# Four inner projections and the cross queries computed feature-major, inputs laid out transposed, and a new order table, in a two-layer decoder trunk

## The chip, the cores and the metric

The kernel runs on one core of a Trainium2 chip. The metric is the time of one execution in microseconds (us), taken on the device. The engines are TensorE (PE, matrix products; PEld is its loading of stationary operands), VectorE (DVE), ScalarE (ACT), GpSimd (POOL) and SyncE (SP), which here issues nearly all transfers. Sums of products land in PSUM, a small memory of eight banks beside PE; everything else is in SBUF.

## The reference

Two decoder layers on x (1, 256, 1024) with a memory `mem` (1, 256, 1024), all float32. Each layer:

```
x = LN1(a*x + 0.5 * SwiGLU_1(x))                      # hidden width 2816
z = x @ w_in + b_in                                   # split into u, v, cb, cc, ch, the latents of MLA, the inputs of NSA, gates ga..gd
y_A = (u * (causal(w_s) @ LN(v) + b_s)) @ w_out       # gMLP: chunks of 128 tokens, 4 groups of 128 features
y_B = (cb * conv3(cc * ch)) @ w_out                   # gated short conv, 3 taps along the tokens, width 512
y_C = multi-head latent attention                     # MLA, 8 heads, causal
y_D = native sparse attention                         # NSA, 8 heads in 2 groups
x = LN2(a*x + (sum_i sigmoid(g_i) * y_i) @ w_o)
q, k, v = x @ wq, mem @ wk, mem @ wv                  # 4 heads of 128
x = LN3(a*x + softmax(q k^T / sqrt(128)) v @ wo)
x = LN4(a*x + 0.5 * SwiGLU_2(x))
```

## The kernel before

**Tiling.** The 256 tokens are two tiles of 128 (t = 0, 1). An activation is kept token-major (tokens on the 128 partitions) in `x[t]`, and once more transposed, feature-major, as `xh`, `xl` of tile t: eight blocks of 128 features, `xh` the value rounded to fp32r and `xl` the rest. Every weight comes from HBM once, as float32, in pieces of up to 512 KB: `unit` (L221) issues the transfer of a piece to `raw` on SP (L233), ACT rounds it to `wh` (L236) and DVE subtracts to `wl` (L237). There are 4 `raw` buffers and 8 pairs of `wh`, `wl`. A product is three matmuls, written out in `mm3` (L246): high by high (L248), high by low (L249), low by high (L250). They add into one PSUM tile.

**z and its transposes.** `z` (L407) computes a group of columns of x @ w_in token-major: for each t and each of eight k, a 128x128 block of `xh` is the stationary operand and 512 columns of weights move. The bias is a row of b_in that a transfer spreads over all partitions (256 KB for 512 columns); DVE adds it while it empties PSUM. Where a result is needed feature-major, PE transposes it: a matmul of 128 columns by the identity `ident`, four of them into one PSUM tile (`transposes`, L294; every such row of the trace has L298), and ACT and DVE split the copy into high and low. That is so for the product u * s of the gMLP (`zu`), for cc * ch (`zch`) and the gate cb (`zcb`) of the conv, for the cross queries (`xq`), for the merged sum of the branches (`T`, into `xh`, L286), for MLA's queries and keys (`mq`, `mk`), for softmax results (`e`), for the normalised x, and for x and mem as loaded (`memr`).

**Stages.** Of a layer: the first FFN (`ffn`, L366), `mixing` (L747) with its four branches a to d, gates and `w_o`, then the keys of mem (`xattn_k`, L873; 96 matmuls of 256 columns, the weights stationary and the transposed mem moving), LN2 (`layer_norm`), the cross attention (`xattn`, L900: queries for both t, scores, softmax, the values of mem in `xattn_v`, outputs, then `xattn_wo` through `wide`), LN3 and the second FFN with LN4. `run` (L941) loads x on SP in three parts after the first weight piece and transposes it on PE, four blocks of four.

**What sets the order.** The program is written stage by stage, and then each engine's instructions are put into the order of a table of numbers, `ISSUE` (L984), that holds for PE, ACT, DVE, POOL and SP: `issue_order` (L969) adds a dependence from each instruction to the next of its engine. Nothing is decided at run time; an instruction that waits holds up all that stand behind it on its engine.

Of the kernel before, what the change touches and what calls it, by code (L numbers as in the profile page):

```python
# [17 lines left out]
P = 128  # L18
# [43 lines left out]
IN_COLS, ZW = _in_columns()  # L62
WOUT_ROWS = np.arange(512).reshape(2, 4, 64).transpose(1, 0, 2).reshape(-1)
# [9 lines left out]
def _constants():  # L73
# [31 lines left out]
    for j in range(4):  # L105
# [24 lines left out]
        "b_in": IN_WIDTH, "gmlp_ln_g": 512, "gmlp_ln_b": 512, "mla_qnorm_g": 256, "mla_kvnorm_g": 128}  # L130
# [7 lines left out]
SMALL = {"ws": 512, "bs": 4, "cw": 12, "pek": 16, "pev": 16, "wck": 1024, "wcv": 1024}  # L138
# [18 lines left out]
DEFER = 3  # L157


class Build:  # L160
    def __init__(self, ctx, tc, aps):
# [10 lines left out]
        self.ident = self.p.tile([P, P], F32, name="ident")  # L172

# [47 lines left out]
    def unit(self, W, l, k0, nk, c0, w):  # L221
# [3 lines left out]
        with self.tc.high_priority(offset=WPRI):  # L225
# [3 lines left out]
            pieces = []  # L229
            for k in range(0, nk, kp):  # L230
                m = min(kp, nk - k) * w
# [6 lines left out]
                pieces.append((hi, lo))  # L238

        def get(k, n0, n1):  # L240
            i, r = divmod(k, kp)
            hi, lo = pieces[i]
            return hi[:, r * w + n0:r * w + n1], lo[:, r * w + n0:r * w + n1]
# [57 lines left out]
    def big(self, t, name, kt=KD):  # L301
        h = self.p.tile([P, KD, P], F32R, name=self.nm("xh"), tag=f"xh{t}", bufs=1)
        lo = self.p.tile([P, KD, P], F32R, name=self.nm("xl"), tag=f"xl{t}", bufs=1)
        return h, lo

    def to_xT(self, t, x, scale=1.0):
        h, lo = self.big(t, "x")
# [58 lines left out]
    def ffn(self, l, which, lnw, last=False):  # L366
# [3 lines left out]
        for gi in range(6):  # L370
            c0 = gi * 512
            w = min(512, FF - c0)
            if w == 512:
                u1 = self.cols(w1, l, c0, w, KD)
                u3 = self.cols(w3, l, c0, w, KD)
            else:
                u13 = self.cols((w1, w3), l, c0, 2 * w, KD)
            for t in range(NT):
                self.stream = "af"[t]
                if w == 512:  # L380
# [3 lines left out]
                else:  # L384
# [22 lines left out]
    def z(self, l, names, evac):  # L407
# [275 lines left out]
    def gmlp(self, l, S):  # L683
# [12 lines left out]
        def spatial(t):  # L696
            v, u = S["v", t], S["u", t]
            ps = self.acc()
            for i in range(4):
                nc.tensor.matmul(ps[:, i * P:(i + 1) * P], ws[:, i * P:(i + 1) * P], v[:, i * P:(i + 1) * P],  # L700
                                 start=True, stop=True, skip_group_check=True)
            for i in range(4):
                sl = slice(i * P, (i + 1) * P)
                nc.vector.scalar_tensor_tensor(u[:, sl], ps[:, sl], bs[:, i:i + 1], u[:, sl], op0=ALU.add,
                                               op1=ALU.mult)

        def turn(t):
            u = S["u", t]
            pt = self.transposes([u[:, i * P:(i + 1) * P] for i in range(4)])
            out[t] = self.pair("ya", pt)  # L710
        self.later += [lambda t=t, f=f: f(t) for f in (spatial, turn) for t in range(NT)]
        return out

    def conv(self, l, S):
        nc = self.nc
        cwv = S["cw"].rearrange("p (f k) -> p f k", f=4)
        out, Z = {}, {}

        def turn(t):
            zp = S["ch", t]  # L720
            nc.vector.tensor_mul(zp, zp, S["cc", t])
            pt = self.transposes([zp[:, i * P:(i + 1) * P] for i in range(4)])
            zt = self.p.tile([P, 4, P + 2], F32, name=self.nm("zpT"), tag="zpT", bufs=2)
            if t == 0:
                nc.vector.memset(zt[:, :, 0:2], 0.0)
            else:
                nc.vector.tensor_copy(zt[:, :, 0:2], Z[0][:, :, P:P + 2])
            nc.scalar.copy(zt[:, :, 2:], pt.rearrange("p (f t) -> p f t", f=4))
            Z[t] = zt

        def taps(t):
            zt = Z[t]
            y = self.s("y")
            yv = y.rearrange("p (f t) -> p f t", f=4)
# [433 lines left out]
```

## Time and profile before

| | |
|---|---|
| median of 3 runs | 1530.36 us (1526.17 to 1535.17) |
| the profiled execution | 1528.15 us, of which the span of the trace is 1526.4 us |
| PE busy | 1489.9 us, 98% of the span |
| DVE, ACT, POOL busy | 1002.8, 719.9 and 50.6 us |
| moved by DMA | 278.76 MB, 183 GB/s over the span |
| mean granted clock of PE | 0.997 |

The span runs from the first to the last instruction that the profiler saw. A row of the trace carries the line of the kernel, the operation, the tiles that it writes and reads, and in brackets the engine's idle time before it with what ended that. Matmuls overlap, so the duration in a row is longer than the distance between the starts of two rows; the distance is what a matmul costs.

### The profile page before, as it was taken

How to read it: one execution, taken by the hardware profiler on the slowest of the kernel's cores; microseconds unless marked ns; L12 is line 12 of the kernel's file. 1: busy time of each engine (PE TensorE's matmuls, PEld its weight loads, DVE VectorE, ACT ScalarE, POOL GpSimd, SP SyncE). 2: the span in 40 equal slices, each digit the busy share in tenths (PEclk: the TensorE clock that was granted, in tenths of full speed). 3: DMA queues.
4: the chain of work that ended last, by engine and by line, in shares of the span. 5: the costliest groups of instructions: out<-in, count | busy, mean ns of one | idle time of the engine just before them, and what ended most of it. 6: DMA issues, size and time to landing. Idle time of an engine off the chain costs nothing.

```text
span 1526.4 us, 20113 instructions
## 1 busy us (share of the span) xinstructions
PE 1489.9 (98%) x7606; PEld 1234.3 (81%) x7606; DVE 1002.8 (66%) x1426; ACT 719.9 (47%) x1060; POOL 50.6 (3%) x48
## 2 busy tenths in 40 slices
PE   8999999999999999999999999999999999999997
PEld 6888888877887888888878888888778878888886
DVE  5545478878866767554565556788887577765644
ACT  6435344555644454544345444355565444544541
POOL 0000001000120000000000000010001100000000
PEclk9999999999999999999999999999999999999999
DMA  7567557424475545566555666654245655356551
GB/s 275 163 222 238 192 185 243 139 90 151 151 235 204 181 162 166 178 196 206 166 193 183 197 213 201 219 202 159 98 139 185 221 193 193 124 195 205 184 189 69
DMA packets 83473, 278.76 MB, mean 183 GB/s; under 512 B 10288, under 2 KB 11952, under 8 KB 83376
## 3 DMA queue, kind: packets, MB, share of 16 engines
q1 hardware_dynamic: 83232, 277.41, 55.2%
q8 instruction: 60, 0.98, 0.3%
q14 instruction: 37, 0.30, 0.1%
q10 hardware_dynamic: 144, 0.07, 0.0%
HBM read 276.39 MB, written 1.05 MB: 182 GB/s over the span
## 4 chain that ended last, share of the span: by engine, by line
PE 88%; DMA 4%; DVE 3%; ACT 3%; issue 1%; SPq 0%; POOLq 0%; POOL 0%; ACTq 0%; DVEq 0%
PE acc L248 22%; PE acc L250 22%; PE acc L249 22%; PE oacc L248 4%; PE oacc L249 4%; PE oacc L250 4%; PE tr L298 3%; DMA raw<-in_wflat_dram 3%; DVE wl L237 2%; ACT wh L236 2%; PE att L474 2%; PE oacc L487 1%; PE acc L298 1%; PE acc L935 1%; PE att L919 0%
## 5 line engine op out<-in xcount | busy, mean ns | idle before, releaser
L236 ACT CAST wh<-raw 128x1024 fp32r<-128x1024 f32 (+2 forms) x486 | 501.4, 1041 | 518.5 <-PE acc L250 330.1
L237 DVE TENSOR_TENSOR wl<-raw,wh 128x1024 fp32r<-128x1024 f32 (+2 forms) x486 | 583.4, 1212 | 239.4 <-ACT wh L236 230.0
L248 PE MATMUL acc<-wh,xh 128*128 128x512 f32 (+2 forms) x1168 | 461.3, 396 | 8.5 <-ACT xh L286 4.2
L250 PE MATMUL acc<-wh,xl 128*128 128x512 f32 (+2 forms) x1168 | 454.9, 390 | 0.1
L249 PE MATMUL acc<-wl,xh 128*128 128x512 f32 (+2 forms) x1168 | 454.5, 390 | 0.0
L248 PEld LDWEIGHTS acc<-wh,xh 128*128 128x128 f32 x1168 | 220.0, 188 | 52.3 <-ACT xh L283 6.0
L250 PEld LDWEIGHTS acc<-wh,xl 128*128 128x128 f32 x1168 | 219.8, 188 | 44.3 <-DVE xl L284 1.6
L249 PEld LDWEIGHTS acc<-wl,xh 128*128 128x128 f32 x1168 | 220.2, 189 | 39.9 <-issue 0.2
L248 PE MATMUL acc<-wh,hh 128*128 128x512 f32 x264 | 103.0, 390 | 0.0
L250 PE MATMUL acc<-wh,hl 128*128 128x512 f32 x264 | 102.8, 389 | 0.0
L249 PE MATMUL acc<-wl,hh 128*128 128x512 f32 x264 | 102.7, 389 | 0.0
L391 DVE SCALAR_TENSOR_TENSOR h<-acc,sil 128x512 f32<-128x512 f32 (+1 forms) x28 | 17.2, 614 | 98.2 <-PE acc L250 94.0
L249 PE MATMUL oacc<-wl,xh 128*128 128x512 f32 x176 | 68.7, 390 | 0.0
L248 PE MATMUL oacc<-wh,xh 128*128 128x512 f32 x176 | 68.7, 390 | 0.0
L250 PE MATMUL oacc<-wh,xl 128*128 128x512 f32 x176 | 68.5, 389 | 0.0
L319 POOL TENSOR_TENSOR rstd<-var,cst 128x1 f32<-128x1 f32 x28 | 23.6, 846 | 1112.2 <-DVE var L318 1111.9
L250 PEld LDWEIGHTS acc<-wh,hl 128*128 128x128 f32 x264 | 49.6, 188 | 10.3
L248 PEld LDWEIGHTS acc<-wh,hh 128*128 128x128 f32 x264 | 49.5, 188 | 10.2
L249 PEld LDWEIGHTS acc<-wl,hh 128*128 128x128 f32 x264 | 49.6, 188 | 10.1
L389 ACT ACTIVATE sil<-acc 128x512 f32<-128x512 f32 (+1 forms) x48 | 27.0, 563 | 53.6 <-PE acc L250 53.6
L449 ACT ACTIVATE e<-att,nm 128x256 f32<-128x256 f32 (+1 forms) x112 | 46.9, 430 | 8.7 <-DVE nm L445 8.7
L481 ACT COPY pT<-tr 128x512 f32<-128x512 f32 x36 | 21.1, 586 | 46.2 <-PE tr L298 45.9
(251 smaller groups left out, 1724.8 us busy)
## 6 DMA issues: line engine op xcount, KB each, us to landing
raw<-in_wflat_dram SPq DMA_DIRECT2D x466, 512.0 KB, 5.1
bias<-in_rows_dram SPq DMA_DIRECT2D x30, 256.0 KB, 5.8
lng<-in_rows_dram SPq DMA_DIRECT2D x8, 512.0 KB, 6.9
lnb<-in_rows_dram SPq DMA_DIRECT2D x8, 512.0 KB, 7.3
raw<-in_wflat_dram SPq DMA_DIRECT2D x8, 416.0 KB, 4.5
wc<-in_small_dram SPq DMA_DIRECT2D x8, 256.0 KB, 7.1
memr<-in_mem_dram SPq DMA_DIRECT2D x8, 256.0 KB, 6.7
raw<-in_wflat_dram SPq DMA_DIRECT2D x4, 420.0 KB, 3.6
```

The source lines that it names most:

```text
L236: nc.scalar.copy(hi[:, :m], raw[:, :m])
L237: nc.vector.tensor_sub(lo[:, :m], raw[:, :m], hi[:, :m])
L248: mm(out, ah, bh, start=start, stop=False, skip_group_check=True)
L249: mm(out, ah, bl, start=False, stop=False, skip_group_check=True)
L250: mm(out, al, bh, start=False, stop=stop, skip_group_check=True)
L298: self.nc.tensor.transpose(t[:rows, i * part:(i + 1) * part], s, self.ident[:part, :part])
L319: nc.gpsimd.tensor_tensor(y, v, self.c("mhalf"), op=ALU.pow)
L389: nc.scalar.activation(sil, pa, AF.Silu)
L391: nc.vector.scalar_tensor_tensor(h, pb, 0.5, sil, op0=ALU.mult, op1=ALU.mult)
L449: nc.scalar.activation(e[:, h * keys:(h + 1) * keys], ps[:, h * keys:(h + 1) * keys], AF.Exp, bias=nm[:, h:h + 1], scale=scale, accum_out= ...
L474: nc.tensor.matmul(ps[:, i * nk + s * P:i * nk + (s + 1) * P], qT(h0 + i), kT(h0 + i, s), start=True, stop=True, skip_group_check=True)
L481: nc.scalar.copy(pTs[-1], pt)
```

## The change

**Feature-major products.** A new function, `turned`, replaces `z` for u, cc, ch and cb, and the token-major query product: the stationary operand is a 128x128 block of weights, and both token tiles move, 256 columns in two blocks of 128 (`both`; `xh` and `xl` are now one tile for both t). The result is feature-major, 128 features by 256 tokens, two such halves in a PSUM tile. The bias is a column of one number per partition (`bcol`), taken along by the instruction that empties PSUM; gmlp_bs becomes a row spread over the partitions. `gmlp` and `conv` are rewritten for that layout: the spatial product of the gMLP has v stationary and w_s moving, and the conv's taps run over 256 tokens at once. The transposes of zu, zch, zcb and xq are not in the program any more.

**Layout.** mem and x come from the host transposed as well (`memt`, `xt`); their transposes on PE are not in the program any more. x is also loaded token-major, later, for LN1. `xt` is first on SP's queue, `ident` comes on SP after it instead of on ACT's, and the first weight piece is cut into two of 256 KB.

**The start.** Ten float32 matmuls of 128x128 on a tile of zeros (`WARM`, tile `warm`) stand first on PE. The first FFN group computes both t for each k in turn.

**Cross attention.** The keys are made in two pieces, each of two heads with its own weight unit: the first is written ahead of w_o's code, the second behind it. The values are made in two pieces too, one for each tile of mem: the first ahead of the queries, the second behind the scores. `xattn_wo` is written out for each t in turn.

**Counts.** PE's program had 7124 matmuls: 5496 of 512 columns, 208 of 256, 852 of 128x128, the rest of other shapes. It now has 7502: 5016, 1168 and 750. `ISSUE` is new for all five engines.

The diff, without the tables and cut to its core:

```
 def unit(...):
+            steps = [(k, min(kp, nk - k)) for k in range(0, nk, kp)]
+            if self.woff == P * n:
+                steps = [(0, 1), (1, 1)] + steps[1:]
...
+    def both(self, k):
+        return self.xh[:, :, k, :], self.xl[:, :, k, :]
...
+    def turned(self, W, l, c0, evac, src, units=None):
+        us = units or self.cols(W, l, c0, 512, KD)
+        for b in range(2):
+            a = self.acc()
+            for f in range(2):
+                i = 0
+                for nk, get in us:
+                    for k in range(nk):
+                        o = (2 * b + f) * P
+                        self.mm3(a[:, f * SEQ:(f + 1) * SEQ], *get(k, o, o + P), *src(i), i == 0, i == KD - 1)
+                        i += 1
+                        if i == DEFER:
+                            self.flush()
+            evac(b, a)
...
 def gmlp(...):
-                nc.tensor.matmul(ps[:, i * P:(i + 1) * P], ws[:, i * P:(i + 1) * P], v[:, i * P:(i + 1) * P],
-            pt = self.transposes([u[:, i * P:(i + 1) * P] for i in range(4)])
-            out[t] = self.pair("ya", pt)
+                    nc.tensor.matmul(ps[:, (i * NT + t) * P:(i * NT + t + 1) * P], S["v", t][:, f * P:(f + 1) * P],
+                                     ws[:, f * P:(f + 1) * P], start=True, stop=True, skip_group_check=True)
...
+                nc.vector.scalar_tensor_tensor(sp[j][:, sl], a[:, sl], self.bias("u", 2 * j + i), sp[j][:, sl],
+                                               op0=ALU.add, op1=ALU.mult)
+            out[j] = self.pair("ya", sp[j])
+        self.turned("w_in", l, ZW["u"][0], gated, self.both)
...
 def conv(...):
-            pt = self.transposes([zp[:, i * P:(i + 1) * P] for i in range(4)])
-            pt = self.transposes([cb[:, i * P:(i + 1) * P] for i in range(4)])
+        for n, f in (("cc", first), ("ch", second), ("cb", third)):
+            self.turned("w_in", l, ZW[n][0], f, self.both)
...
 def mixing(...):
         self.load_memT()
+        self.xattn_k(l, 0)
         out = self.wide("w_o", l, KD, lambda t, k: (MT[t][0][:, k, :], MT[t][1][:, k, :]), (4,))
...
 def load_memT(...):
+        for q in range(KD // 2):
+            r = self.s("memr")
+            nc.sync.dma_start(r, self.a["memt"][:, q * 512:(q + 1) * 512])
+            h, lo = self.s("memh", dt=F32R), self.s("meml", dt=F32R)
+            self.split(r, h, lo)
...
 def xattn(...):
+        self.xattn_v(l, 0)
+        self.turned("xattn_wq", l, 0, keep, self.both)
...
+        self.xattn_v(l, 1)
...
 def run(self):
-            nc.scalar.dma_start(self.ident, self.a["consts"][:, :P])
-            nc.sync.dma_start(self.x[0][:, :512], self.a["x"][:P, :512])
-            nc.sync.dma_start(self.x[0][:, 512:], self.a["x"][:P, 512:])
-            self.xT = [self.to_xT(0, self.x[0])]
+        warm = self.p.tile([P, P], F32, name="warm")
+        nc.vector.memset(warm, 0.0)
+        a = self.acc()
+        for i in range(WARM):
+            nc.tensor.matmul(a[:, :P], warm, warm, start=True, stop=True, skip_group_check=True)
+        for q in range(2):
+            for t in range(NT):
+                h, lo = self.big(t)
+                r = self.s("xr")
+                nc.sync.dma_start(r, self.a["xt"][:, t * D + q * 512:t * D + (q + 1) * 512])
+                sl = slice(4 * q, 4 * q + 4)
+                self.split(r.rearrange("p (k t) -> p k t", k=4), h[:, sl, :], lo[:, sl, :])
+        nc.sync.dma_start(self.ident, self.a["consts"][:, :P])
+        for t in range(NT):
+            nc.sync.dma_start(self.x[t], self.a["x"][t * P:(t + 1) * P, :])
...
             out, g, b = self.mixing(l)
-            self.xattn_k(l)
+            self.xattn_k(l, 1)
```

**The order on PE, three places.** A row names the line, the tile written and the tiles read (with running numbers of the program), and the columns; x4 stands for four alike. `mm3` has lines 256 to 258 after, `transposes` 306. First the very start. Before, PE begins with a transpose of x:

```order
L298 MATMUL tr_70<-ident,x_63 128x128 x4
L248 MATMUL acc_150<-wh_104,xh_68 128x512
L249 MATMUL acc_150<-wl_105,xh_68 128x512
L250 MATMUL acc_150<-wh_104,xl_69 128x512
...
L248 MATMUL acc_150<-wh_110,xh_68 128x512
L298 MATMUL tr_77<-ident,x_63 128x128 x4
```

After:

```order
L997 MATMUL acc_69<-warm 128x128 x10
L256 MATMUL acc_154<-wh_102,xh 128x512
L256 MATMUL acc_156<-wh_102,xh 128x512
L257 MATMUL acc_154<-wl_103,xh 128x512
L258 MATMUL acc_154<-wh_102,xl 128x512
L256 MATMUL acc_154<-wh_108,xh 128x512
```

The transposes are gone, the matmuls on zeros stand in their place, and two sums (one for each t) alternate over the first weight piece.

Second, the up-projection of MLA in the first layer, where its queries and keys (`mq`, `mk`) are transposed; `att` are products of its latents, `yah` and `ybh` belong to the outputs of the gMLP and conv branches. Before:

```order
L248 MATMUL att_2641<-wh_2593,lh_1951 128x384
L249 MATMUL att_2641<-wl_2594,lh_1951 128x384
L250 MATMUL att_2641<-wh_2593,ll_1952 128x384
L298 MATMUL tr_2619<-ident,mq_2611 96x128 x4
L298 MATMUL tr_2634<-ident,mk_2630 96x128 x4
L248 MATMUL att_2663<-wh_2599,lh_1951 128x512
```

After:

```order
L256 MATMUL acc_3972<-wh_3968,ybh_3506 128x512
L257 MATMUL acc_3972<-wl_3969,ybh_3506 128x512
L306 MATMUL tr_2621<-ident,mq_2613 96x128 x4
L258 MATMUL acc_3972<-wh_3968,ybl_3507 128x512
L256 MATMUL acc_3932<-wh_3888,xh 128x512
L257 MATMUL acc_3932<-wl_3889,xh 128x512
```

The transposes of mq and mk, which stood together right behind the up-projection, now stand apart from it and from each other, among matmuls of the conv's output and of a gate; the transpose of mk (tr_2636) follows 28 rows behind that of mq.

Third, the start of w_o in the first layer; `oCh`, `oCl` are the outputs of MLA, whose product with mla_wout is the last branch, and `T` the merged sum. Before:

```order
L248 MATMUL acc_4349<-wh_4300,oCh_2931 128x512
L249 MATMUL acc_4349<-wl_4301,oCh_2931 128x512
L250 MATMUL acc_4349<-wh_4300,oCl_2932 128x512
L298 MATMUL tr_4366<-ident,T_3372 128x128 x4
L298 MATMUL tr_4373<-ident,T_3549 128x128 x4
L248 MATMUL acc_4444<-wh_4450,xh_4364 128x512
L249 MATMUL acc_4444<-wl_4451,xh_4364 128x512
```

After, the first transpose of T, and eleven rows behind it the first rows of w_o:

```order
L258 MATMUL acc_4468<-wh_4422,oCl_2934 128x512
L256 MATMUL acc_4483<-wh_4428,oCh_2933 128x512
L306 MATMUL tr_4498<-ident,T_3561 128x128 x4
L257 MATMUL acc_4483<-wl_4429,oCh_2933 128x512
L258 MATMUL acc_4483<-wh_4428,oCl_2934 128x512
```

```order
L257 MATMUL acc_4483<-wl_4435,oCh_2933 128x512
L258 MATMUL acc_4483<-wh_4434,oCl_2934 128x512
L256 MATMUL acc_4617<-wh_4623,xh 128x512
L257 MATMUL acc_4617<-wl_4624,xh 128x512
L257 MATMUL acc_4453<-wl_4429,oCh_2816 128x512
```

The transpose of the first half of T now stands among the last branch's matmuls, and w_o starts on that half (its first four k) with the rest of the branch behind its first two rows.

Two more moves are told in words. The second transpose block of MLA and the softmax blocks `e` of the layer's attention have matmuls of the conv and the gates ahead of them. And between the last matmul of w_o and the first of the queries now stand 67 matmuls of the keys (256 columns), 24 of the values (512 columns) and three blocks of transposes of x; before, the transposes of x and the queries followed the last matmul of the keys directly.

## Rows read from the trace of the kernel before

**Rows 1.** The page: span, and busy time of each engine.
```profile
span 1526.4 us, 20113 instructions
PE 1489.9 (98%) x7606; PEld 1234.3 (81%) x7606; DVE 1002.8 (66%) x1426; ACT 719.9 (47%) x1060; POOL 50.6 (3%) x48
```

**Rows 2.** Waits of PE: waiting line, what ended it, us in total, times, longest.
```profile
PE tr L298 <- DMA x<-in_x_dram: 6.1, 1, 6.1
PE acc L248 <- ACT xh L286: 4.2, 2, 2.3
PE acc L248 <- ACT xh L283: 4.0, 8, 1.1
PE tr L298 <- ACT mk L661: 2.8, 3, 0.9
PE tr L298 <- DVE e L458: 1.9, 2, 1.8
PE att L474 <- ACT e L449: 1.7, 1, 1.7
PE acc L298 <- DVE y L742: 1.0, 1, 1.0
...
PE att L248 <- ACT mq L650: 0.8, 3, 0.3
...
PE tr L298 <- DVE mq L432: 0.7, 1, 0.7
```

**Rows 3.** Windows: us, busy PE, PEld, DVE, ACT, POOL; clock, DMA share, GB/s.
```profile
325.00:345.00 20.00, 16.79 (x129) 12.80 (x128) 16.54 (x44) 11.03 (x30) 0.00 (x0) 0.91 0.11 27
484.00:494.00 10.00, 8.08 (x43) 6.61 (x42) 8.09 (x11) 5.42 (x7) 0.00 (x0) 1.00 0.65 243
1244.00:1252.00 8.00, 6.08 (x27) 5.08 (x28) 4.92 (x7) 3.67 (x7) 0.00 (x0) 0.79 0.21 75
```

**Rows 4.** Timeline of PE around mem's keys: start, us, line, operation.
```profile
484.62 0.39 PE L249 MATMUL acc<-wl,oCh 128*128 128x512 f32 x1
...
488.93 0.39 PE L250 MATMUL acc<-wh,oCl 128*128 128x512 f32 x1
...
495.41 0.40 PE L250 MATMUL acc<-wh,xl 128*128 128x512 f32 x1
495.64 0.60 PE L298 MATMUL tr<-ident,memr 128*128 128x128 f32 x4
496.00 0.48 PE L248 MATMUL acc<-wh,xh 128*128 128x512 f32 x1
496.31 0.60 PE L298 MATMUL tr<-ident,memr 128*128 128x128 f32 x4
...
516.74 0.28 PE L248 MATMUL acc<-memh,wh 128*128 128x256 f32 x1
...
528.13 0.28 PE L250 MATMUL acc<-memh,wl 128*128 128x256 f32 x1
```

**Rows 5.** Timeline of the first 10 us, all engines (SPq: SP's issues).
```profile
0.74 0.39 SPq L233 DMA_DIRECT2D raw<-in_wflat_dram  x1
...
5.41 1.05 ACT L236 CAST wh<-raw 128x1024 fp32r<-128x1024 f32 x1 [2.96 <-DMA raw<-in_wflat_dram]
...
6.14 1.09 PE L298 MATMUL tr<-ident,x 128*128 128x128 f32 x4 [6.14 <-DMA x<-in_x_dram]
...
7.91 0.79 PE L248 MATMUL acc<-wh,xh 128*128 128x512 f32 x1 [0.68 <-ACT xh L283]
...
9.35 0.63 PE L248 MATMUL acc<-wh,xh 128*128 128x512 f32 x1
...
9.78 0.63 PE L249 MATMUL acc<-wl,xh 128*128 128x512 f32 x1
```

**Rows 6.** Groups by line and tile: the transposes of mem, with their count.
```profile
L298 PE MATMUL tr<-ident,memr x32: 270/272/273, 495.6 to 1254.8; 128*128 128x128 f32 x32
```

**Rows 7.** The chain that ended last: DVE's row behind the last matmul.
```profile
1518.07 0.70 DVE x L351
```

More of the change, by code (lines that the diff above doesn't have):

```diff
@@ L228, in unit @@
             kp = max(1, 1024 // w)
-            pieces = []
-            for k in range(0, nk, kp):
-                m = min(kp, nk - k) * w
+            steps = [(k, min(kp, nk - k)) for k in range(0, nk, kp)]
+            if self.woff == P * n:
+                steps = [(0, 1), (1, 1)] + steps[1:]
+            pieces = {}
+            for k, kn in steps:
+                m = kn * w
                 raw = self.p.tile([P, 1024], F32, name=self.nm("raw"), tag="raw", bufs=RAW_BUFS)
@@ L731, in taps, with first @@
[L731 to L734, printed above, removed]
-            for f in range(4):
-                nc.vector.tensor_scalar(yv[:, f, :], zt[:, f, 0:P], cwv[:, f, 0:1], None, op0=ALU.mult)
+        out, cc, y = {}, {}, {}
+        z = self.p.tile([P, 4, SEQ + 2], F32, name=self.nm("zpT"), tag="zpT", bufs=1)
+        nc.vector.memset(z[:, :, 0:2], 0.0)
+        def first(j, a):
+            cc[j] = self.s("cc")
+            for i in range(2):
+                sl = slice(i * SEQ, (i + 1) * SEQ)
+                nc.scalar.activation(cc[j][:, sl], a[:, sl], AF.Identity, bias=self.bias("cc", 2 * j + i))
@@ L737, in taps, with second @@
+        def second(j, a):
+            y[j] = self.s("y")
+            for i in range(2):
+                f = 2 * j + i
+                sl = slice(i * SEQ, (i + 1) * SEQ)
+                nc.vector.scalar_tensor_tensor(z[:, f, 2:], a[:, sl], self.bias("ch", f), cc[j][:, sl],
+                                               op0=ALU.add, op1=ALU.mult)
+                nc.vector.tensor_scalar(y[j][:, sl], z[:, f, 0:SEQ], cwv[:, f, 0:1], None, op0=ALU.mult)
                 for k in (1, 2):
-                    nc.vector.scalar_tensor_tensor(yv[:, f, :], zt[:, f, k:k + P], cwv[:, f, k:k + 1], yv[:, f, :],
+                    nc.vector.scalar_tensor_tensor(y[j][:, sl], z[:, f, k:k + SEQ], cwv[:, f, k:k + 1], y[j][:, sl],
@@ L739, in taps, with third @@
                                                    op0=ALU.mult, op1=ALU.add)
-            cb = S["cb", t]
-            pt = self.transposes([cb[:, i * P:(i + 1) * P] for i in range(4)])
-            nc.vector.tensor_mul(y, pt, y)
-            out[t] = self.pair("yb", y)
-        self.later += [lambda t=t, f=f: f(t) for f in (turn, taps) for t in range(NT)]
+        def third(j, a):
+            for i in range(2):
+                sl = slice(i * SEQ, (i + 1) * SEQ)
+                nc.vector.scalar_tensor_tensor(y[j][:, sl], a[:, sl], self.bias("cb", 2 * j + i), y[j][:, sl],
+                                               op0=ALU.add, op1=ALU.mult)
+            out[j] = self.pair("yb", y[j])
@@ L857, in load_memT @@
         nc = self.nc
+        self.memT = []
         self.stream = "f"
[L859 to L871 removed]
@@ L937, in xattn @@
                                          skip_group_check=True)
-            oT[t] = self.pair("xo", ob)
-        return self.wide("xattn_wo", l, 4, lambda t, k: tuple(z[:, k * P:(k + 1) * P] for z in oT[t]), (2,))
+            oT = self.pair("xo", ob)
+            if t == 0:
+                us = [self.unit("xattn_wo", l, k, 2, 0, D) for k in (0, 2)]
+            out[t] = [self.acc(), self.oacc() if t == 0 else self.acc()]
+            for n in range(2):
+                for k in range(4):
+                    self.mm3(out[t][n], oT[0][:, k * P:(k + 1) * P], oT[1][:, k * P:(k + 1) * P],
+                             *us[k // 2][1](k % 2, n * 512, n * 512 + 512), k == 0, k == 3)
+        return out
     def run(self):
```

187 lines of the change are left out of this document (88 added, 99 removed), and 319 rows, old and new, of the table ISSUE.

## The prediction

> **What bounds the kernel now.** I read the page's totals first. TensorE (PE) is busy 1489.9 of 1526.4 us [rows 1]; the reader is to see that no other engine comes near (DVE 66%, ACT 47%), so the time moves only if matmul time or PE's idle 36.5 us moves. PE's waits come next [rows 2]: 6.1 us go by before the first matmul, and after the last one DVE's final addition starts at 1518.07 [rows 7], so 8.3 us follow it. That leaves 36.5 − 6.1 − 8.3 = 22.1 us of holes, 0.7 of them at the head; the waits name the rest: the merged mixer state on its way to w_o (4.2), normalised rows on their way to the next product (4.0, the head's 0.7 in it), MLA's keys (2.8), the softmax `e` (1.9 and 1.7), and smaller ones. The windows [rows 3] add what no idle row shows: from 325 to 345 the granted clock averages 0.91 and from 1244 to 1252 0.79, though it is 1.00 elsewhere. 20 × 0.09 / 0.5 = 3.6 and 8 × 0.21 / 0.5 = 3.4 us at the lower level (1.2 instead of 2.4 GHz); each such stretch loses half of itself, about 1.7 us. Both follow a run of waits for `e` or the 2.3 us wait for w_o's state. The 484 to 494 stretch, with the shorter of the two waits on that row (4.2 − 2.3 = 1.9), stayed at 1.00.
>
> **Durations of a step.** A matmul of 512 columns: from 484.62 to 488.93 there are 19 steps, 0.2267 us each. One of 256 columns: from 516.74 to 528.13 there are 95 steps, 0.120 each [rows 4]. Four 128-column transposes between two matmuls: from the matmul at 495.41 to the block at 496.31 lie two matmuls and one block of four, 0.90 − 2 × 0.227 = 0.447 us [rows 4].
>
> **Transposes that go: −10.7.** The u, conv and query tiles come out of PE already feature-major, mem comes transposed from memory. Per program 96 transposes go outside the head: the 32 of mem [rows 6], and 16 each of u, of the conv's product, of its gate cb and of the queries. 24 blocks × 0.447 = −10.7. None is hidden: PE is busy around them. The ACT and DVE copies behind them go too, off the path.
>
> **Matmuls that are cut in two: +6.4.** The same products are now issued with the weight slice held and both token tiles moving: 480 matmuls of 512 columns become 960 of 256. 480 × (2 × 0.120 − 0.2267) = +6.4. The nearest row is mem's keys, which has the same shape and loads stationary data for every matmul [rows 4]; but its moving operand is one block, here it is two blocks of 128. Bounds: at half of a 512 step (0.1134) it costs 0, and a gain is excluded, since the same columns stream; a 256 step is 0.0067 dearer than that half, and if the second block pays this once more (an estimate) it is 0.127 and +12.8. I take +6.4, by the row of the same shape.
> The Trainium skill, "TensorE: Matmul & The Clock Gate", section "Back-to-back issue gap", gives N/2.4 + 2.5 ns for an isolated matmul: 109 ns and 216 ns, so two halves would cost 2.5 ns per pair, +1.2 in all, and the sum would be 5.2 lower. It says itself that this falls short for small N in a stream with weight loads; the trace agrees, 0.120 where the formula has 0.109, and I keep the rows.
>
> **The head: −4.0.** Before, the first weight piece is issued at 0.74 and its cast starts at 5.41; x, issued behind it, is waited for until 6.14, then four transposes, a cast, and the first weight matmul at 7.91; the steps 9.35 to 9.78 take 0.43, twice the full-clock step [rows 5]. Now x arrives transposed, first on its queue, and the first weight piece is halved: the cast at about 5.2, first matmul at 6.1 to 6.5, −1.4 to −1.8. Three more x transpose blocks among the first matmuls go, 3 × 0.447 = −1.3. Some six steps lie at half clock, 6 × 0.2 = 1.2; ten matmuls on zeros stand in the time that PE otherwise idles away, and they cost nothing, because PE waits for data anyway; if they do what the row of half-speed steps suggests, the 1.2 goes. Sum −4.0 to −4.3; without the last part −2.7. I take −4.0. If the two x halves and the smaller first pieces arrive later than x did, the first matmul is bound by data as before.
>
> **Holes: −11.** What fills each hole is read from the order of the instructions. MLA's transposes of mq and mk had nothing ahead of them but the product they depend on; now between 5 and 28 matmuls (1 to 6 us) of the conv branch and of the gate stand there, where 0.7 to 0.9 is waited for: its rows 2.8 + 0.7 + 0.8 go. The transposes of the merged state stood directly ahead of w_o's first matmul; now the first ones stand twelve matmuls (2.6 us) earlier among the last branch's, against a wait of at most 2.3 [rows 2]: 4.2 go. Softmax's `e` now has about 4.5 us of other matmuls beside a chain that lasted 4.2 or more in the trace (an estimate: 2.4 to 2.9 of matmuls that stand there in the order, plus the 1.7 to 1.8 waited); those two rows, 3.6, just go. The conv transposes' wait of 1.0 goes with them. Between w_o and the queries now stand a part of K and of V, 67 + 24 matmuls (14 us), where about 1.6 us of the 4.0 was waited for. Together 14.7 of 21.4 us goes, 6.7 stays (the starts of the FFN, the second normalisation). A new order makes new waits in places that this trace can't show. Bounds: 0, if the cover is enough everywhere, and 14.7, if every wait reappears elsewhere. I take 3, about half of what stays, nearer to 0 because the fillers are longer than the waits. So 21.4 becomes about 10: −11.4.
>
> **Clock: −3.4.** With the waits on `e` and on w_o's state gone, the two slow stretches lose their occasion: −1.7 each. Bounds 0 and −3.5.
>
> **Rest: −0.4 and 0.** At the end [rows 7] both additions of the last normalisation now run while Pool takes the root; that hides one, about −0.4 (bounds 0 and −0.7, the row's own length). ACT and DVE have fewer copies and take the biases along as columns: nothing, hidden by PE, since both are far from full [rows 1]. Eight broadcast bias rows of 256 KB leave SP's queue, two for the gMLP and the head's smaller pieces come: nothing, with DMA at 0.65 in the fullest of the three windows [rows 3]; uncovered, one late piece costs a wait of up to 4.7 us, which the first piece took from issue to cast [rows 5].
>
> **Sum.** 1526.4 − 10.7 + 6.4 − 4.0 − 11.4 − 3.4 − 0.4 = 1502.9. The profiled run took 1528.15, 1.75 over its span: 1504.7; the median of the runs shown lies 2.2 above that run: 1507.
>
> **Rivals.**
> A, the holes only move, that is, the new order doesn't do what it says: each filler is drawn from another place, and holes and clock stay as they are. For: 36.5 us of idle are already only 2%, and filler taken from the branches is missing later. Against: the K and V pieces and the gate matmuls have no urgent reader. 1526.4 − 10.7 + 6.4 − 4.0 − 0.4 = 1517.7, median 1522.
> B, slower: the moving operand in two blocks of 128 is taken as two passes. Price: the block of four transposes gives 0.112 per 128 columns, so 0.224 instead of 0.120, 960 × 0.104 = +100: 1607. It makes the kernel slower than before from (0.120 + 23.4/960) = 0.144 us per matmul, measurably so from 0.152. For: no row of before moves two blocks. Against: in both shapes measured here a step is set by its columns (0.44 ns per column at 512, 0.47 at 256 [rows 4]), so the second block would have to cost a whole pass more; hence the small chance.
> C, the head's gain and the clock's don't come (first matmul bound by data as before, a stretch falls again): +1.3 + 3.4, about 1511.
>
> **How the numbers follow.** The forecast has 0.66, A 0.16, C 0.12, B 0.06. The predicted time is the forecast's, 1507. The range goes down to 1498, the step cost nearer its lower bound and no new waits (−6.4 and −3), and up to 1521: the halves at their upper bound (1513), C (1511), and most of A. Outside lie B, a part of A and the tails, under 2 in 10. A measurement of this kernel tells about 0.5% from no change, so faster means under 1522.7 and slower over 1538. Faster: the forecast, C and two thirds of A, less the tails, 0.86; same 0.08; slower 0.06.
>
> **What would show it.** In the profile after: matmuls of 256 columns in u and the conv at 0.120 (B: over 0.15); 98% busy PE on a span of some 1503; first weight matmul at 6.1 to 6.5 and steps of 0.23 right behind it; no wait over 0.5 us for mk, for `e` or for w_o's state; granted clock 1.00 in both stretches; K and V matmuls where the query wait was. Wrong is the forecast if holes sum to over 13 us between head and tail, if the halves take over 0.13, or if PE waits for weight pieces, which no row of its waits names now.

## The result

The changed kernel takes 1517.89 us (median of 5 runs, 1516.17 to 1518.77), against 1530.36 before: 0.9914 of it, with a 95% interval of 0.989 to 0.9937. The forecast was 1507, with a range of 1498 to 1521. So it went the way that was forecast, inside the range, but with 12.5 us of the 23.4 that the sum had. Spans and waits below are those of one profiled run of each kernel: that of the changed kernel was the slowest of its five (1518.77), that of the kernel before lay 2.2 below its median, so the two spans differ by 9.4 only.

The page after, its span and busy times (before: [rows 1]):

```profile
span 1517.0 us, 20797 instructions
PE 1488.4 (98%) x7994; PEld 1243.5 (82%) x7994; DVE 999.5 (66%) x1390; ACT 715.6 (47%) x1061; POOL 52.8 (3%) x48
```

What PE waited for, after (line, what ended the wait, us in total, times, longest; before: [rows 2]):

```profile
PE acc L256 <- ACT wh L244: 4.3, 5, 1.9
PE acc L257 <- DVE wl L245: 2.3, 3, 1.7
PE acc L256 <- DVE zzc L801: 2.1, 2, 1.5
PE acc L256 <- DVE zv L801: 1.8, 2, 0.9
PE tr L306 <- DVE mq L466: 1.4, 2, 0.9
PE acc L976 <- ACT xpT L972: 1.4, 2, 0.7
PE acc L256 <- ACT xoh L291: 1.4, 2, 0.7
PE oacc L256 <- ACT wh L244: 1.3, 3, 0.7
PE acc L997 <- DVE zpT L765: 1.1, 1, 1.1
PE tr L306 <- DVE e L492: 0.9, 2, 0.7
PE tr L306 <- DVE T L870: 0.8, 1, 0.8
PE oacc L257 <- DVE wl L245: 0.7, 2, 0.5
```

The reader is to see that the names have changed. The long rows of before (w_o's state, `mk`, `e`, the conv's `y`) are gone or small, and in their place stand waits for weights, 4.3 + 2.3 + 1.3 + 0.7 = 8.6 us (1.9 of them for the first piece), where before had 0.3, and waits for PSUM to be emptied (`zzc`, `zv`), 3.9.

The two spans, cut at the first weight matmul and the last matmul (holes are PE's idle time between them; the busy time is what is left):

| us | before | after | five raw buffers, before | five raw buffers, after |
|---|---|---|---|---|
| to the first weight matmul | 7.9 | 7.1 | 8.0 | 7.4 |
| holes | 21.3 | 18.1 | 15.6 | 10.2 |
| busy | 1488.8 | 1484.2 | 1489.4 | 1480.9 |
| behind the last matmul | 8.3 | 7.5 | 8.3 | 7.5 |
| span | 1526.4 | 1517.0 | 1521.3 | 1506.1 |

The two columns on the right belong to experiments below.

### The profile page after: what moved, and what is told of

Read it like the earlier page. It is cut to its first block, busy times and chain, and to the rows that moved or that the text cites. A ratio compares the mean times of both kernels' runs of the same rounds, so it can differ in the third digit from the quotient of the medians.

```text
span 1517.0 us, 20797 instructions
## 1 busy us (share of the span) xinstructions
PE 1488.4 (98%) x7994; PEld 1243.5 (82%) x7994; DVE 999.5 (66%) x1390; ACT 715.6 (47%) x1061; POOL 52.8 (3%) x48
## 4 chain that ended last, share of the span: by engine, by line
PE 85%; DMA 7%; DVE 4%; ACT 2%; issue 1%; SPq 0%; POOL 0%; DVEq 0%; ACTq 0%
PE acc L256 21%; PE acc L258 21%; PE acc L257 21%; DMA raw<-in_wflat_dram 6%; PE oacc L257 4%; PE oacc L256 4%; PE oacc L258 4%; PE tr L306 4%; DVE wl L245 3%; ACT wh L244 2%; PE att L508 2%; PE oacc L521 1%; PE att L256 1%; PE att L258 1%; PE att L257 1%
## 5 line engine op out<-in xcount | busy, mean ns | idle before, releaser
L245 DVE TENSOR_TENSOR wl<-raw,wh 128x1024 fp32r<-128x1024 f32 (+4 forms) x487 | 585.6, 1220 | 289.8 <-ACT wh L244 280.9
L244 ACT CAST wh<-raw 128x1024 fp32r<-128x1024 f32 (+4 forms) x487 | 499.7, 1040 | 410.9 <-PE acc L258 247.8
L256 PE MATMUL acc<-wh,xh 128*128 128x512 f32 (+2 forms) x1008 | 389.8, 393 | 6.7 <-ACT wh L244 4.3
L257 PE MATMUL acc<-wl,xh 128*128 128x512 f32 (+2 forms) x1008 | 389.5, 390 | 0.6 <-DVE wl L245 0.6
L258 PE MATMUL acc<-wh,xl 128*128 128x512 f32 (+2 forms) x1008 | 388.3, 389 | 0.0
L256 PEld LDWEIGHTS acc<-wh,xh 128*128 128x128 f32 x1008 | 188.5, 188 | 48.5 <-ACT wh L244 8.5
L256 PE MATMUL acc<-wh,hh 128*128 128x512 f32 x264 | 100.7, 396 | 0.0
L256 PE MATMUL acc<-xh,wh 128*128 128x256 f32 x320 | 90.8, 287 | 2.0 <-DVE zv L801 1.8
L257 PE MATMUL acc<-xl,wh 128*128 128x256 f32 x320 | 90.4, 285 | 0.0
L258 PE MATMUL acc<-xh,wl 128*128 128x256 f32 x320 | 90.0, 284 | 0.0
L256 PE MATMUL oacc<-wh,xh 128*128 128x512 f32 x176 | 69.7, 396 | 0.6 <-ACT wh L244 0.6
L256 PEld LDWEIGHTS acc<-xh,wh 128*128 128x128 f32 x320 | 61.0, 192 | 3.1 <-issue 2.5
L257 PEld LDWEIGHTS acc<-xl,wh 128*128 128x128 f32 x320 | 61.2, 191 | 0.6 <-issue 0.3
L258 PEld LDWEIGHTS acc<-xh,wl 128*128 128x128 f32 x320 | 61.2, 192 | 0.1
L256 PEld LDWEIGHTS acc<-wh,hh 128*128 128x128 f32 x264 | 49.0, 188 | 13.9 <-ACT wh L244 4.9
```

Of the source, the lines that this page charges most:

```text
L244: nc.scalar.copy(hi[:, :m], raw[:, :m])
L245: nc.vector.tensor_sub(lo[:, :m], raw[:, :m], hi[:, :m])
L256: mm(out, ah, bh, start=start, stop=False, skip_group_check=True)
L257: mm(out, ah, bl, start=False, stop=False, skip_group_check=True)
L258: mm(out, al, bh, start=False, stop=stop, skip_group_check=True)
```

## The experiments

All times, with the ratio to the kernel before on the same chip:

| kernel | us | ratio, 95% interval |
|---|---|---|
| the change | 1517.89 | 0.9914 [0.9890, 0.9937] |
| warm0: no zeros | 1518.32 | 0.9919 [0.9901, 0.9938] |
| warm19: nineteen | 1521.80 | 0.9942 [0.9922, 0.9963] |
| before_halves | 1535.04 | 1.0030 [1.0012, 1.0049] |
| before_memt | 1528.06 | 0.9989 [0.9976, 1.0002] |
| after_merge | 1528.43 | 0.9998 [0.9981, 1.0014] |
| after_fix | 1529.31 | 0.9994 [0.9983, 1.0006] |
| after_bias | 1519.79 | 0.9921 [0.9899, 0.9943] |
| before_raw5 | 1522.90 | 0.9948 [0.9930, 0.9965] |
| after_raw5 | 1509.29 | 0.9859 [0.9837, 0.9882] |
| after_raw6 | 1507.30 | 0.9850 [0.9836, 0.9865] |
| raw5_fix | 1518.31 | 0.9914 [0.9897, 0.9932] |
| raw5_three | 1510.64 | 0.9877 [0.9860, 0.9893] |

### The start: fewer and more zeros

```
-WARM = 10
+WARM = 0        # and the ten entries out of PE's table
```

> The ten matmuls on zeros are left out; the output does not depend on them. Theory (the start is bound by the arrival of x and weight pieces, so the zeros give nothing): first weight matmul at 7.1 us as with them, some eight steps of 0.42, and by 32 us as many weight matmuls started as with the zeros (90 in the trace); time 1518 within 2 us. Rival (the zeros lift the clock and save part of the slow steps): 1 to 2 us slower and behind at 32 us.

```
-WARM = 10
+WARM = 19       # and nine entries more at the head of PE's table
```

> Nineteen matmuls on zeros in place of ten, so that PE is busy until the first weight piece is cast (about 7.1 us) instead of pausing for 1.9 us. Theory: the clock holds, the steps right behind 7.1 take 0.23 instead of 0.42, but PE then waits for the next weight pieces, and by 32 us it stands where it stood (about 90 weight matmuls): time within 1 us of 1518. Rival (clock-bound start): the 1.3 us of slow steps are gained for good, 1516.5.

PE's timeline of the changed kernel at its start (start, us, line, operation; x2 is two alike): a pause of 1.89 behind the zeros, then steps of 0.42 to 0.43 (8.32, 8.75, 9.17).

```profile
7.13 0.73 PE L256 MATMUL acc<-wh,xh 128*128 128x512 f32 x2 [1.89 <-ACT wh L244]
...
8.32 0.63 PE L258 MATMUL acc<-wh,xl 128*128 128x512 f32 x1
8.75 0.63 PE L256 MATMUL acc<-wh,xh 128*128 128x512 f32 x1
9.17 1.05 PE L257 MATMUL acc<-wl,xh 128*128 128x512 f32 x2
```

Without zeros the same steps come at the same places; with nineteen there is no pause and the steps are 0.23 from the start. First warm0, then warm19:

```profile
7.32 1.22 PE L256 MATMUL acc<-wh,xh 128*128 128x512 f32 x2 [7.32 <-ACT wh L244]
8.34 0.63 PE L257 MATMUL acc<-wl,xh 128*128 128x512 f32 x1
8.76 0.63 PE L258 MATMUL acc<-wh,xl 128*128 128x512 f32 x1
```

```profile
1.05 6.68 PE L997 MATMUL acc<-warm 128*128 128x128 f32 x38 [1.05 <-DVE zpT L765]
7.48 0.71 PE L256 MATMUL acc<-wh,xh 128*128 128x512 f32 x2
8.03 0.40 PE L257 MATMUL acc<-wl,xh 128*128 128x512 f32 x1
8.27 0.39 PE L258 MATMUL acc<-wh,xl 128*128 128x512 f32 x1
```

So the zeros can hold the clock, if there are enough of them to leave no pause; ten don't, and the changed kernel would lose nothing without them (1518.32). But the held clock isn't kept as time. By the trace's records (of which some can be missing) warm19 has started 36 weight matmuls by 16 us and warm0 31; by 32 us they have 99 and 101. What warm19 gained it gave back in one wait of 0.97 us for a weight piece at 23.4. That is the theory of a start bound by arriving data; that both stood at 99 to 101 at 32 us, where I expected 90, is a miss in the number: the profiled run of the changed kernel itself lost some 1.6 us in three waits there, and so stood at 90, no further than the kernel before (90). Its window of 16 to 32 us shows it (start:end, us, busy PE, PEld, DVE, ACT, POOL, granted clock, DMA share, GB/s); in the kernel before and in warm0 PE is busy for all 16.00 there:

```profile
16.00:32.00 16.00, 14.45 (x61) 10.83 (x59) 9.87 (x9) 9.74 (x11) 0.00 (x0) 1.00 0.79 264
```

warm19 as a whole took 1521.80, where the theory had 1518 within 1 us: that number was missed. Why it is slower isn't settled: in its profiled run the wait for `zzc` in the second layer was 2.4 us, and nothing that comes from the start was seen to reach so far.

### The price of a half, and of a transpose

The kernel before, with the 480 matmuls cut in two and the same orders. Its sums aren't the reference's; the instructions and bytes are those meant.

```
+        if halves:
+            one = mm
+            def mm(o, a, b, **kw):
+                one(o[:, :256], a, b[:, :256], **kw)
+                one(o[:, 256:], a, b[:, 256:], **kw)
```

> The kernel before with the 480 matmuls of u, cc, ch, cb and the queries each cut into two of 256 columns, the stationary operand loaded for each, all else and all orders as before. Theory (steps of 0.120 as for mem's keys): 480 x 0.0133 = 6.4 us more, 1536.8, and steps of 0.120 in these stretches. Rival one (half of a 512 step plus 2.5 ns per pair): 1.2 us more. Rival two (the second load of the stationary operand shows): over 0.13 a step, over 12 us more.

+4.4 us to the kernel before in the same comparison (1530.67), with an interval of 1.8 to 7.5: the term of +6.4 is inside, the +1.2 of the formula outside. The steps are 0.120 there too: eight of them lie between 255.72 and 256.68. In the changed kernel, where the moving operand comes in two blocks, they are the same; two rows of a stretch without a break, 108 steps apart, give (1055.55 − 1042.59) / 108 = 0.120:

```profile
1042.59 0.28 PE L258 MATMUL acc<-xh,wl 128*128 128x256 f32 x1
...
1055.55 0.28 PE L258 MATMUL acc<-xh,wl 128*128 128x256 f32 x1
```

The Trainium skill, "TensorE: Matmul & The Clock Gate", section "Back-to-back issue gap", gives N/2.4 + 2.5 ns for an isolated matmul, which makes an estimate of 109 ns at 256 columns; the measurement decides, and it's 120 in every form that was run here.

The kernel before, with mem transposed from memory:

```
-            ps = self.transposes([mt[t, kk // 4][:, kk % 4 * P:(kk % 4 + 1) * P] for kk in (k, k + 1)
-                                  for t in range(MEM // P)])
-            self.split(ps, h, lo)
+            self.split(r, h, lo)
```

> The kernel before with one part of the change: mem comes transposed from memory, its 32 transposes are not in PE's program, all else and all orders as before. Theory (a block of four transposes costs 0.447 us of a busy PE): 8 x 0.447 = 3.6 us less, 1526.7, and the stretch from the start of w_o to the end of the keys shorter by 1.8 us in each layer. Rival (they filled holes): the hole ahead of w_o or of the queries grows instead, less than 1 us gained.

PE's timeline of before_memt in the first layer: the first matmul of w_o, one that waits for a weight piece, and the last of the keys.

```profile
493.69 0.50 PE L248 MATMUL acc<-wh,xh 128*128 128x512 f32 x1 [1.50 <-ACT xh L286]
...
500.88 0.50 PE L249 MATMUL acc<-wl,xh 128*128 128x512 f32 x1 [0.53 <-DVE wl L237]
...
528.73 0.28 PE L250 MATMUL acc<-memh,wl 128*128 128x256 f32 x1
```

That is 35.04 us, where the kernel before took 528.13 [rows 4] − 492.11 = 36.02: 0.98 less for four blocks, not 1.8. The rest came back as the wait for `wl`, which the kernel before doesn't have there: two steps, of 0.91 and 0.34 where 0.23 is usual, make 0.79. Without them it is 1.77, 0.44 a block, as the rows had it. So the price held, and a new wait took nearly half of it back, in part as the rival said. In the second layer it's 37.63 against 35.03, 2.60 less, with the same new wait (0.55); there the wait ahead of w_o was 1.42 instead of 2.32 and the clock didn't fall behind it, so a fallen clock had cost 2.60 − 0.98 = 1.62 us. The kernel before shows that price by itself. Its first ten rows from w_o on are the same in both layers, and take 2.60 us in the first and 4.20 in the second, 1.60 more:

```profile
492.11 0.50 PE L248 MATMUL acc<-wh,xh 128*128 128x512 f32 x1 [1.92 <-ACT xh L286]
...
494.71 0.40 PE L250 MATMUL acc<-wh,xl 128*128 128x512 f32 x1
...
1245.92 0.50 PE L248 MATMUL acc<-wh,xh 128*128 128x512 f32 x1 [2.32 <-ACT xh L286]
...
1250.12 0.39 PE L250 MATMUL acc<-wh,xl 128*128 128x512 f32 x1
```

The time as a whole, −2.6 with an interval of −3.7 to +0.3, takes in both the theory and the rival and doesn't decide.

### PE's order at w_o undone

```
 PE, changed:  ... oC, tr_4498<-T, oC x11, w_o, w_o, oC x11, w_o ...
 PE, here:     ... oC x23, tr_4498<-T, w_o, w_o, w_o ...
```

> The changed kernel with one part of PE's order undone: the first transposes of the merged state and the first rows of w_o stand behind the last matmul of the fourth branch again, in both layers. Theory (the filler hides this chain): a wait of 1 to 2.3 us ahead of w_o in each layer, 2 to 4.6 us more in all, and a granted clock of 0.5 for some 3 us behind it if the pause has the length of the one at 1246 us of the kernel before (up to 1.7 us more). Rival (holes only move): the wait comes back but later waits for w_o's weight pieces shrink by as much, within 1 us.

+10.5, twice what the theory had. ACT, DVE and PE ahead of w_o in the second layer:

```profile
1241.64 0.60 ACT L294 ACTIVATE xh<-tr 128x512 fp32r<-128x512 f32 x1 [9.26 <-PE tr L306]
...
1242.78 0.69 DVE L292 TENSOR_TENSOR meml<-memr,memh 128x512 fp32r<-128x512 f32 x1 [6.99 <-ACT memh L291]
...
1244.81 0.47 PE L256 MATMUL acc<-wh,xh 128*128 128x512 f32 x1 [3.21 <-DVE T L865]
```

The transpose was moved on PE alone. ACT's copy of it kept its place in ACT's queue, so ACT sat 9.26 us behind it with casts of mem and of weights waiting, and DVE 6.99 behind ACT. PE then waited 3.21 and the clock fell, as the windows of 4 us say:

```profile
1244.00:1248.00 4.00, 2.70 (x8) 1.65 (x8) 3.86 (x7) 3.05 (x4) 0.00 (x0) 0.76 0.07 17
1248.00:1252.00 4.00, 3.34 (x10) 2.88 (x11) 4.00 (x5) 0.60 (x1) 0.00 (x0) 0.50 0.61 210
```

So with ACT's and DVE's orders as they are, the place of PE's transposes among the filler keeps this chain and the weight casts moving, and taking them out of it isn't made good later: that holes only move falls at this place. What the filler is worth with the other engines' orders fitted to the old place, this run doesn't tell. Not all of the 10.5 belongs to it; the wait for `zzc` in the first layer was 2.6 in this profiled run, 1.1 more than in the changed kernel's.

### The new waits mended, twice

```
 DVE, changed:  wl_2080, wl_2086, wl_2092, zzc_1772, zzc_1799
 DVE, here:     zzc_1772, wl_2080, wl_2086, zzc_1799, wl_2092     # the same in layer 2
 and later on DVE: ws behind three wl; r, mq ahead of two wl; T ahead of one wl
```

> Eight entries of DVE's order moved: the additions that empty PSUM of the latents (zzc) ahead of a weight subtraction that waits for its cast, the masking of w_s behind three weight subtractions, one part of MLA's rotation and one sum of the merged state ahead of a weight subtraction. Theory (the new order made these waits: 1.53 and 0.58 on zzc, 1.67 on wl behind w_s, 0.90 on mq, 0.81 on T): they go, 4 to 5.5 us less, about 1513. Rival (weights arrive too late anyway): the time comes back as waits for wh and wl, at most 1 us less.

It became slower by 11.4. In the changed kernel, the rows on which the repair rested, DVE and PE:

```profile
233.93 1.23 DVE L245 TENSOR_TENSOR wl<-raw,wh 128x1024 fp32r<-128x1024 f32 x1 [1.96 <-ACT wh L244]
235.07 1.08 DVE L801 TENSOR_TENSOR zzc<-acc,bias 128x416 f32<-128x416 f32 x2
```

```profile
235.71 0.40 PE L256 MATMUL acc<-wh,xh 128*128 128x280 f32 x1 [1.53 <-DVE zzc L801]
```

`zzc` looks ready and stuck behind a subtraction that waits. With it moved ahead, second layer:

```profile
992.31 0.59 DVE L801 TENSOR_TENSOR zzc<-acc,bias 128x416 f32<-128x416 f32 x1 [9.86 <-DMA bias<-in_rows_dram]
...
1005.07 0.81 DVE L801 TENSOR_TENSOR zzd<-acc,bias 128x280 f32<-128x280 f32 x2 [4.06 <-DMA bias<-in_rows_dram]
```

```profile
1008.02 1.09 PE L306 MATMUL tr<-ident,zza 128*128 128x128 f32 x4 [7.20 <-DVE zza L466]
```

The addition needs a bias row that SP issues late, and its 9.86 us now held up three weight subtractions and with them the raw buffers. In the changed kernel's second layer that bias row was issued at 980.95 and took 5.67 to land, until 986.62; the first `zzc` ran at 986.64, right behind the subtraction. Both had ended together, and the row shows only one of them. The three other moves did what they should: no wait for `T` or w_s is left in after_fix, and for `mq` only 0.5.

```
 SP:   bias (zc) two weight pieces earlier, in both layers
 DVE:  zzc one weight subtraction earlier; the other three moves as above
```

> The changed kernel with four raw buffers, and on SP the bias row of the latents two weight pieces earlier in both layers (in the second with one small transfer that stands ahead of it); on DVE the additions zzc one weight subtraction earlier, and the masking of w_s, the rotation and the sum of the merged state placed as in the first mended order. Theory (the first mended order failed because zzc waited for its bias row on DMA and held the weight subtractions behind it): with the row there in time the waits on zzc (2.1), w_s (1.67), mq (0.9) and T (0.8) shrink by 4 or more, 1513. Rival (what binds is the supply of weight pieces, whoever waits): within 2 us of 1518.

1519.79, not better than the change: the rival. The waits for `zzc`, w_s and `T` are gone from PE's list, but weights have 7.8 where they had 8.6, and the rotation's `zza` has 4.4: it stands on DVE behind `zzd`, which at 994.30 had waited 2.70 for the next small bias row. So the number is the rival's, but not its reason alone: the wait moved to another late transfer, and weight pieces are only part of that.

### A fifth raw buffer, in both kernels

```
-RAW_BUFS = 4
+RAW_BUFS = 5
-SF_BUFS = 17
+SF_BUFS = 15
```

`RAW_BUFS` counts the buffers `raw` that the weight pieces land in; `SF_BUFS` counts working tiles, given up for the room.

> As the kernel with DVE's order mended, and with five raw weight buffers in place of four, so that five transfers can be under way (two buffers of the side stream are given up for the room). Theory (the remaining waits for weight pieces, some 7 us in the changed kernel with those at 24 to 32, 663, 769 and 1437 us, come from four transfers under way with about 5 us from issue to landing): they shrink to under 3, about 4 us less than with the order alone, 1509. Rival (the DMA engines themselves are full there): no change against the mended order, within 1 us.

> The kernel before with five raw weight buffers in place of four (and two buffers of the side stream fewer), all orders as before. Theory (its order left PE nearly no wait for weights, 0.3 us): no change within 2 us. Rival (four transfers under way limit the kernel before as well, hidden in other waits): 3 us or more less.

> The changed kernel with five raw weight buffers in place of four (and two buffers of the side stream fewer), all orders as they are. Theory (four transfers under way, each some 5 us from issue to landing, hold ACT's and DVE's queues up in both kernels; the kernel before gained 8 us from the fifth buffer): the waits for wh and wl (8.6 us with the 1.67 behind w_s) and part of those for zzc (2.1) shrink, 4 to 8 us less than the changed kernel, about 1512. Rival (the fifth buffer helps only the order of before): within 2 us of 1518.

> The changed kernel with six raw weight buffers in place of four (and four buffers of the side stream fewer), all orders as they are. Theory (with five the supply no longer binds outside the start: the waits for wh there fell from 5.6 to 2.1, all of it at the first piece): no more gain, within 1.5 us of 1509.3. Rival (the supply still binds, unseen in PE's waits): 2 us or more less, under 1507.5.

raw5_fix missed its 1509 because its orders were the bad ones, but it is 11 us faster than the same orders with four buffers (1529.31 to 1518.31); after_raw5 is 8.6 faster than the change, and before_raw5 is 7.8 faster than the kernel before (1530.67). The last was the rival: I had expected nothing, since PE named no weights there. PE's waits in before_raw5, against [rows 2]:

```profile
PE acc L248 <- ACT xh L283: 3.2, 8, 0.7
...
PE acc L248 <- ACT xh L286: 1.6, 2, 0.8
```

No instruction was moved, and the wait for w_o's state fell from 4.2 to 1.6: ACT's copy of that state had stood behind weight casts that waited for their transfers (in the second layer, casts at 1240.92 and 1243.09 waited 1.15 and 1.11, and the copy ran at 1245.28). So a part of the holes of before was the supply of weights under another name. The trace of before had that name, in ACT's list of waits and not in PE's:

```profile
ACT wh L236 <- DMA raw<-in_wflat_dram: 150.3, 100, 4.1
```

With the fifth buffer that row is 46.4 us in 35 waits. In the changed kernel it is, with four buffers and then with five:

```profile
ACT wh L244 <- DMA raw<-in_wflat_dram: 72.0, 63, 4.5
```

```profile
ACT wh L244 <- DMA raw<-in_wflat_dram: 20.6, 18, 4.9
```

SP issues a piece when a subtraction on DVE has freed a buffer (it waited for that 1127.5 us in 439 cases in the changed kernel), and the piece then takes 5.0 us to land. Whether the pieces under way or the time that a buffer is held is what's short, these runs don't separate. In after_raw5 the list of PE begins

```profile
PE acc L256 <- ACT wh L244: 2.1, 1, 2.1
```

and this one wait for `wh` is the first piece of all. Behind it stand `zv` (1.8), `zzc` (1.6), `mq`, `xpT` and `xoh` (1.4 each), nearly as with four buffers. Holes fall from 18.1 to 10.2 and busy time by 3.3, though the instructions are the same. PE's weight loader tells of that part: its idle time ended by `wh` in the group of L256 falls from 8.5 to 4.1, much of it under matmuls that still ran.

With six buffers 1507.30, 2.0 less than with five. That just meets the rival's number, but the two intervals overlap, so it's open whether the sixth adds anything. It is the fastest here, and faster than both kernels.

> The changed kernel with five raw buffers, and on DVE three entries moved that wait for no transfer: the masking of w_s behind three weight subtractions, one part of MLA's rotation and one sum of the merged state ahead of a weight subtraction. Theory (with the supply in hand a wait that is order alone can be taken away): the wait for mq at 1170 us (0.89) goes, w_s and T are hidden already, about 1 us less, 1508.3. Rival (it moves on): within 0.3 us of the time with five buffers, or longer.

1510.64 (1506.05 to 1512.34), against 1509.29: no gain that the runs can tell, though the wait for `mq` fell from 1.4 to 0.5 in PE's list and the profiled span was 1504.3. Inconclusive.

## Why the prediction was right, and where it was too large

The time went the way that was forecast and lies in the range, but that is in good part the range's width: it ran up to 1521 to take in most of rival A, and 1517.9 lies nearer to A's 1522 than to the forecast's 1507. Of the prediction's own signs of being wrong two came: holes sum to 18.1 (over 13), and PE waits for weight pieces (6.7 us outside the first). `e` and the state T also have waits of 0.7 and 0.8, over the 0.5 named. So the account of the holes failed. A isn't the account either: the old holes went and the two slow stretches are at 1.00, but new holes of nearly the same sum came. Term by term:

- **Transposes, −10.7.** Held as a price: 0.44 us a block in the eight that were tried alone, against 0.447. "None is hidden" didn't hold there: 0.8 of the 1.8 us in each layer came back as a wait for a weight piece. The other 16 blocks weren't tried alone.
- **Halves, +6.4.** Held: 0.120 a step, in two blocks as in one. Rival B, two passes, has no trace of support.
- **The head, −4.0.** This failed. The first weight matmul came 0.8 earlier, not 1.6: the first cast of x ran from 4.19, but ACT cast the halved weight piece only at 6.46, behind the second part of x (5.70) in its queue. That queue isn't the whole cause: in warm19 both parts of x were cast by 5.18, and the cast of the weight piece still waited for its transfer until 6.21. The slow steps stayed, since the zeros ended in a pause of 1.9; and what was ahead at 16 us was taken back by waits for weight pieces at 24 to 32 us. Rival C had named it.
- **Holes, −11.4.** This failed by the most, −3.2. Of the 14.7 that were to go most did: 2.8 of `mk`, 3.4 of 4.2 at w_o, 2.7 of 3.6 for `e`, 1.0 for `y`; the rotation's `mq` stayed at 1.4, and the normalised rows fell to 0.2, further than I had it. The step that failed is the 3 us for new waits, "about half of what stays", for which no row stood: they were some 13. 6.7 are for weights outside the first piece (8.6 − 1.9; 1.7 of it is one wait for a subtraction that stands behind the masking of w_s on DVE), 3.9 for `zzc` and `zv`, 2.2 more for `xpT` and `xoh` in the cross attention (1.4 + 1.4, where `xpT` had 0.6), and small ones. With it failed "nothing" for SP's queue and the weights, argued from DMA at 0.65 and from a list in which PE seemed to wait for no weights (0.3 us, a row that [rows 2] leave out). Neither bore on it: with four buffers weight pieces came late, and ACT and DVE carried those waits, 150.3 us of them on ACT before the change. But the buffers explain little of the miss by themselves. With five in both kernels the change brings 13.6 us (1522.90 to 1509.29) where it brings 12.5 with four; against the kernel before on the same chip the ratios are 0.9859 / 0.9948 = 0.9911 and 0.9914. The holes then fall from 15.6 to 10.2, by 5.4 and not by 11.4, and the 7.6 us for `zv`, `zzc`, `mq`, `xpT` and `xoh` are left.
- **Clock, −3.4.** The stretches of [rows 3] are at 1.00 after:

```profile
1228.00:1250.00 22.00, 21.53 (x114) 17.03 (x113) 17.82 (x22) 10.01 (x14) 1.60 (x1) 1.00 0.67 210
325.00:345.00 20.00, 20.00 (x132) 16.29 (x131) 15.65 (x33) 11.54 (x22) 0.00 (x0) 1.00 0.62 199
```

  Over the whole span, only windows of 10 us in the first 20 us lie under 0.995. The mechanism held, in the second layer by its size too: 1.60 against 1.7. The price of the first stretch wasn't measured by itself.
- **The end, −0.4.** It was 0.8, on the same chain: the last addition to x starts at 1509.49 and the span ends 7.5 later.

```profile
1509.49 0.70 DVE x L361
```

By medians the sum was 10.9 short, by the two profiled spans 14.1: holes 8.2; the head's start and slow steps 2.0; the end −0.4; and 4.3 in busy time, of which the clock of the second stretch explains 0.1. The rest may be time that goes with a wait but isn't in its idle row: in before_memt a wait listed with 0.53 made two steps 0.79 longer, and 3.3 us of busy time went with the fifth buffer. That is an inference. A sum that credits each hole of before in full to the new order is too large in any case: with a fifth buffer, and no order changed, the holes of before fell from 21.3 to 15.6.

## What to carry to other kernels

A list of waits names who came last, not what is scarce: where every engine's order is fixed, a late transfer shows as a wait for whatever stands behind its cast. Before a reordering is priced, one more buffer in the load path of the kernel before tells how much of its holes is order and how much is supply; the waits of the engine that casts the weights show it as well, though that engine is far from full. And an instruction moved ahead on an in-order engine brings its other inputs along; each of them has to be looked up, the transfer of a small row too, and each engine that copies its result has to be moved with it.

## What the runs showed of the hardware

A merging addition on POOL and DVE hold each other up. In the changed kernel two weight subtractions beside two such additions take 4.24 us, where two take 2.36 alone just before, and the wait of 0.90 for `mq` stands behind them:

```profile
1171.28 2.36 DVE L245 TENSOR_TENSOR wl<-raw,wh 128x1024 fp32r<-128x1024 f32 x2
...
1174.62 3.53 POOL L870 TENSOR_TENSOR T<-T,T 128x512 f32<-128x512 f32 x2 [21.70 <-DVE T L865]
1174.99 4.24 DVE L245 TENSOR_TENSOR wl<-raw,wh 128x1024 fp32r<-128x1024 f32 x2
```

The Trainium skill, "SBUF — State Buffer", section "SBUF: two separate sides", has DVE and GpSimd lock a shared pair of ports for a whole instruction, also for a DVE operation with two inputs in SBUF. The trace agrees that the second to begin is held, and shows both sides: here POOL began first and DVE lost 1.88 us; at 1150.71 an addition took 2.20 beside a subtraction that had begun at 1150.55 and kept its 1.22, where an addition that began first takes 1.28 to 1.30 (375.36, 398.35).

The granted clock of the record and the steps disagree at the very start: the kernel before and warm0 have 1.00 there with steps of 0.42 to 0.43, which is half of full speed.
